# Issuing the context stream's weight loads from ScalarE's queue instead of SyncE's

## The chip, the cores and the metric

The kernel runs on one core of one Trainium2 chip. The metric is the device time of one execution in microseconds (us), as the median of several runs. Engines are named as in the profile: PE is TensorE's matmul side and PEld its weight load, DVE is VectorE, ACT is ScalarE, POOL is GpSimd, SP is SyncE. SPq and ACTq are the instruction streams of SP and ACT where they issue DMAs.

## The reference

Two blocks run one after the other on a sequence of 256 tokens with D = 1024, all in float32.

```
first block:  h = modulate(rms_norm(x));  x += w_out(dilated attention(h) | differential attention(h))
              h = modulate(rms_norm(x));  x += moe_ffn(h)      # 32 experts, top 4 of them per token, d_ff 1024
              expert:  gu = h @ w_gate_up[e];  g = min(gu_g, 7);  u = clip(gu_u, -7, 7)
                       y  = (g * sigmoid(1.702 g) * (u + 1)) @ w_down[e]
second block: 2 layers over x and a second stream "context" (256 tokens); each layer:
              h = modulate(rms_norm(.)); attention (x also sees the context's K and V),
              a gated MLP branch and a convolution branch, each gated and merged, then w_out;
              then a feed-forward block of 4096 with a squared relu
              the context stream itself is needed through layer 0 only
```

The context's layer 0 does not depend on the first block at all; only the second block's attention needs its K and V.

## The kernel before

A `Builder` class writes the program for a tile scheduler, which places each instruction on its engine's queue by priority and by its own estimate of time. Phase 1 (`build`, from L1766) runs the first block: `front` (attention), `route` (top 4, sort, groups of tokens) and `moe`. While it runs, the whole of the context's layer 0 is put between its steps as filler: `ctx_pass` (L1421) is a generator, and `prio` (L1755) advances it by a listed number of steps (tables FRONT, ROUTE, MOE) behind each step of the first block, whose instructions have the higher priority. While the context's code is written, the flag `self.side` is true (`run_ctx` in `build`). When the generator ends, `self.solo` is set and the experts have the chip alone. Phase 2 then runs the two layers of the main stream, `layer(0)` and `layer(1)`.

In the profiled execution the stages lie so: front 0 to about 285 us, route to about 320, the context beside the experts 345 to 1245, the experts alone 1250 to 1590, the two layers 1590 to the end.

Three helpers carry the context's weights. `load_w` (L317) loads a block of 1024 x 512 float32 weights (2 MB). While `self.side` is true it does so in four DMAs of 512 KB, each into a buffer from `half()` (L297): three of four into one of three `raws` buffers, the fourth into the one `rawx`. The DMA's line is L330, and its queue is `q`, chosen in L319; no caller in the context's code passes one. `wsplit` (L335) makes two operands of each 128 x 512 row of the block: ACT copies it to fp32r as `whis` (L342), and DVE subtracts that from the row to get the rest, `wlos` (L343), with three buffers of each. When both splits of a `raws` buffer's two rows are done, the buffer is free for the next load. `lin_steps` (L354) uses each row in twelve matmuls on PE (L365, tile `side`): for each of four column groups the activation's high part on `whis`, its low part on `whis`, and its high part on `wlos`.

The experts' weights take another road. `load_gu` (L941, DMA at L947) loads an expert's gate and up weights in four DMAs of 2 MB and `load_dn` (L952, DMA at L958) its down weights in two, into two `raw` buffers and one `raw3`, used in turn; all from SP. They are float32 and go to PE without a split: L981 (tile `mlin` or `main`) multiplies gate and up, `swiglu` (L917) runs on DVE (L920 to L925) with one tanh on ACT (L923, tile `et`), PE transposes (L987), ACT copies the result to `aT` (L989), L1006 multiplies by the down weights, and ACT puts the outcome into `y` (L1042). The index of each expert is loaded into a register of SP (`value_load` in `expert_base`), so the experts' DMAs can be issued by SP alone as the code stands.

At the end of phase 1 two blocks of layer 0 are loaded ahead with `self.tail` true and `self.side` false; and phase 2 uses `load_w` with `self.side` false throughout.

Of the kernel before, what the change touches and what calls it, by code (L numbers as in the profile page):

```python
# [98 lines left out]
class Builder:  # L99
# [216 lines left out]

    def load_w(self, w, q=None):  # L317

        q = q or self.nc.sync  # L319
        small = self.side  # L320
        if self.tail:
            self.nblock += 1
            small = self.nblock % 3 == 0
        whole = None if small else self.t(self.raw, [P, 4096], tag="raw")
        rows, k0 = [], 0
        for h in (1, 1, 1, 1) if small else (2, 2):
            n = 2 * h
            r = self.half() if small else whole[:, k0 * 512:(k0 + n) * 512]
            r = r.rearrange("p (k n) -> p k n", k=n)
            q.dma_start(r, w[:, k0:k0 + n, :])  # L330
            rows += [r[:, i:i + self.wn, :] for i in range(0, n, self.wn)]
            k0 += n
        return rows
# [1547 lines left out]
```

## Time and profile before

| | |
|---|---|
| median of 3 runs | 2759.27 us (2755.33 to 2763.97) |
| the profiled execution, its own time | 2754.71 us |
| span from its first to its last instruction | 2752.8 us |
| mean granted clock of TensorE over the span | 0.977 of full speed |
| PE busy | 2592.5 us, 94% of the span |
| DVE, ACT, POOL busy | 1626.1, 1157.5, 322.2 us |
| bytes moved by DMA | 769.80 MB |

The busy times are sums over the whole span; they say nothing yet of which engine sets the pace in which stage. For that, the trace is cut into the stages named above. Waits are listed as pairs: the instruction that waited, then the work that ended its wait.

### The profile page before, as it was taken

What the parts mean: (1) busy time and instruction counts of PE and PEld (TensorE: products, weight loads), DVE (VectorE), ACT (ScalarE), POOL (GpSimd) and SP (SyncE); (2) the same over time, 40 slices, a digit from 0 to 9 for tenths busy, and PEclk for the clock granted to TensorE, in tenths of its full rate; (3) what the DMA queues carried; (4) which work ended last, traced back from release to release, by engine and by line L of the source; (5) the groups of instructions that cost most, each with busy time, mean ns of one, the idle gap of its engine ahead of it and who ended that gap; (6) DMA issues with size and microseconds to landing.
All of it is one profiled execution on the core that took longest, in us unless ns stands there. A gap on an engine that the chain in (4) does not pass through costs nothing. (4 is left out here: it accounts for less than half of the span.)

```text
span 2752.8 us, 49781 instructions
## 1 busy us (share of the span) xinstructions
PE 2592.5 (94%) x20358; PEld 2047.0 (74%) x20359; DVE 1626.1 (59%) x3090; ACT 1157.5 (42%) x1987; POOL 322.2 (12%) x334
## 2 busy tenths in 40 slices
PE   7999999999899999999889978899999998999998
PEld 5657877678567777875333477899789987899998
DVE  3465543778554524443121279988546789996655
ACT  2333343333243323431111156765445566656543
POOL 0000000000000000000000025442001055350000
PEclk9989899999999999999999989999999999999999
DMA  9758599989999999999999934326854443344442
GB/s 398 300 226 296 203 401 417 364 347 405 378 357 386 390 361 361 409 419 363 392 392 421 415 129 168 125 105 238 289 203 184 158 180 123 131 146 184 154 184 85
DMA packets 119370, 769.80 MB, mean 280 GB/s; under 512 B 11632, under 2 KB 12016, under 8 KB 52832
## 3 DMA queue, kind: packets, MB, share of 16 engines
q1 hardware_dynamic: 117744, 759.15, 70.6%
q0 software_dynamic: 1392, 7.41, 0.7%
q8 instruction: 162, 2.65, 0.4%
q14 instruction: 72, 0.59, 0.1%
HBM read 762.84 MB, written 3.67 MB: 278 GB/s over the span
## 5 line engine op out<-in xcount | busy, mean ns | idle before, releaser
L343 DVE TENSOR_TENSOR wlo<-raw,whi 128x1024 fp32r<-128x1024 f32 (+1 forms) x288 | 337.6, 1175 | 162.2 <-ACT whi L342 156.6
L365 PE MATMUL lin<-hhi,wlo 128*128 128x256 f32 x1440 | 399.3, 283 | 21.6 <-DVE wlo L343 21.6
L365 PE MATMUL lin<-hhi,whi 128*128 128x256 f32 x1440 | 400.5, 282 | 2.2 <-ACT hhi L284 2.2
L365 PE MATMUL lin<-hlo,whi 128*128 128x256 f32 x1440 | 401.4, 281 | 0.1
L342 ACT ACTIVATE whi<-raw 128x1024 fp32r<-128x1024 f32 (+1 forms) x288 | 276.9, 963 | 257.9 <-PE lin L365 189.3
L981 PE MATMUL mlin<-raw,hG 128*32 128x256 f32 (+2 forms) x2920 | 341.3, 456 | 17.5 <-DMA raw<-in_w_gate_up_dram 17.5
L365 PEld LDWEIGHTS lin<-hhi,wlo 128*128 128x128 f32 x1440 | 269.5, 190 | 37.5 <-DVE wlo L343 33.2
L1585 POOL TENSOR_TENSOR yc<-yc,ctmp 128x256 f32<-128x256 f32 x240 | 252.4, 1075 | 300.6 <-ACT ctmp L1584 300.1
L343 DVE TENSOR_TENSOR wlos<-raws,whis 128x512 fp32r<-128x512 f32 x246 | 166.2, 687 | 196.3 <-ACT whis L342 189.4
L365 PEld LDWEIGHTS lin<-hhi,whi 128*128 128x128 f32 x1440 | 271.0, 189 | 5.8 <-ACT hhi L284 3.7
L365 PEld LDWEIGHTS lin<-hlo,whi 128*128 128x128 f32 x1440 | 272.2, 189 | 3.7 <-issue 2.3
L981 PEld LDWEIGHTS mlin<-raw,hG 128*32 128x32 f32 (+2 forms) x2920 | 129.9, 121 | 178.6 <-issue 110.0
L342 ACT ACTIVATE whis<-raws 128x512 fp32r<-128x512 f32 x246 | 148.9, 627 | 225.6 <-PE side L365 186.2
L365 PE MATMUL side<-hhi,whis 128*128 128x256 f32 x720 | 203.0, 288 | 0.1
L365 PE MATMUL side<-hlo,whis 128*128 128x256 f32 x720 | 199.7, 282 | 0.0
L365 PE MATMUL side<-hhi,wlos 128*128 128x256 f32 x720 | 193.1, 284 | 0.7 <-DVE wlos L343 0.5
L343 DVE TENSOR_TENSOR wlo<-raws,whi 128x1024 fp32r<-128x1024 f32 x108 | 139.0, 1287 | 74.4 <-ACT whi L342 73.8
L1587 DVE SCALAR_TENSOR_TENSOR yc<-gl,cw,yc 128x256 f32<-128x256 f32 x240 | 167.8, 734 | 0.1
L342 ACT ACTIVATE whi<-raws 128x1024 fp32r<-128x1024 f32 x108 | 114.4, 1059 | 118.8 <-PE lin L365 103.8
L1006 PE MATMUL main<-raw,aT 128*32 128x256 f32 (+2 forms) x1408 | 162.6, 453 | 1.1 <-DMA raw<-in_w_down_dram 1.0
L365 PEld LDWEIGHTS side<-hhi,whis 128*128 128x128 f32 x720 | 136.7, 190 | 16.5 <-issue 11.2
L365 PE MATMUL lin<-ahi,whi 128*128 128x256 f32 x528 | 145.7, 279 | 0.0
(603 smaller groups left out, 5737.4 us busy)
## 6 DMA issues: line engine op xcount, KB each, us to landing
raw<-in_w_gate_up_dram SPq DMA_DIRECT2D x120, 2048.0 KB, 11.5
raw<-in_w_down_dram SPq DMA_DIRECT2D x55, 2048.0 KB, 11.1
raw<-in_w_in_dram SPq DMA_DIRECT2D x60, 1024.0 KB, 7.1
raws<-in_w_in_dram SPq DMA_DIRECT2D x95, 512.0 KB, 6.8
raws<-in_w_ff_dram SPq DMA_DIRECT2D x88, 512.0 KB, 8.1
raw<-in_w_ff_dram SPq DMA_DIRECT2D x44, 1024.0 KB, 7.0
phi<-in_ada_w_dram SPq DMA_DIRECT2D x10, 1024.0 KB, 7.4
plo<-in_ada_w_dram SPq DMA_DIRECT2D x10, 1024.0 KB, 7.1
```

What stands on the lines that cost most here:

```text
L342: x = nc.scalar.activation(flat(hi), flat(rows[i]), AF.Copy)
L343: y = nc.vector.tensor_sub(flat(lo), flat(rows[i]), flat(hi).bitcast(F32))
L365: x = nc.tensor.matmul(*args, skip_group_check=True, **kw)
L981: nc.tensor.matmul(d, hT(k), gu[k][c0 // D][:, c0 % D:c0 % D + W], start=False, stop=(k == KC - 1), skip_group_check=True)
L1006: nc.tensor.matmul(pys[h][g * C:(g + 1) * C, :W], st, dn[m][:, c0:c0 + W], start=(m == 0), stop=(m == KC - 1), skip_group_check=True)
L1585: nc.gpsimd.tensor_add(d, d, m)
L1587: self.paced(1, nc.vector.scalar_tensor_tensor(d, x, wcol, d, op0=OP.mult, op1=OP.add))
```

## The change

One line of `load_w` is altered: where no queue is passed and `self.side` is true, the DMA is issued by ACT instead of SP.

```diff
     def load_w(self, w, q=None):
 
-        q = q or self.nc.sync
+        q = q or (self.nc.scalar if self.side else self.nc.sync)
         small = self.side
```

41 calls of `load_w` are made with the flag set, so 164 DMAs of 512 KB (84 MB) change queue. SP's queue goes from 995 instructions to 831, ACT's from 1807 to 1974. The loads of the experts, of the main stream, and of the two blocks loaded ahead stay on SP.

On SP, early in the context stream, the loads of the context's weights (L330) stood between those of the experts (L947, L958; the ISA rows are the register work for the expert's address). The piece of the difference:

```order
 L947 ISA
 L947 DMA raw_6020<-in_w_gate_up_dram 128x2x2048
-L330 DMA raws_3181<-in_w_attn_o_dram 128x1024
-L330 DMA raws_3183<-in_w_attn_o_dram 128x1024
 L947 ISA
 L947 DMA raw_1240_6022<-in_w_gate_up_dram 128x2x2048
-L330 DMA rawx_3185<-in_w_attn_o_dram 128x1024
-L330 DMA raws_3442<-in_w_in_dram 128x1024
 L947 ISA
 L947 DMA raw_6024<-in_w_gate_up_dram 128x2x2048
 L958 ISA
 L958 DMA raw_6112<-in_w_down_dram 128x4096
```

The experts' loads now stand behind one another, and each waits for its own buffer only.

On ACT, at the same place, the splits `whis` of the context's weights (L342) stood so before, each with what it waits for (DMAHW is the arrival of a load, DVE and PE a count of work on these engines):

```order
L342 ACTIVATE whis_3189<-raws_3179 128x512 [waits DMAHW0_49,DVE_49]
L342 ACTIVATE whis_3205<-raws_3179 128x512 [waits DVE_49]
L342 ACTIVATE whis_3221<-raws_3181 128x512 [waits DMAHW2_49,DVE_49]
L342 ACTIVATE whis_3237<-raws_3181 128x512 [waits DVE_49,PE_49]
L342 ACTIVATE whis_3253<-raws_3183 128x512 [waits DMAHW3_49,DVE_49,PE_49]
L342 ACTIVATE whis_3269<-raws_3183 128x512 [waits DVE_49,PE_49]
```

and after the change:

```order
L342 ACTIVATE whis_3189<-raws_3179 128x512 [waits DMAHW0_49]
L342 ACTIVATE whis_3205<-raws_3179 128x512
L330 DMA raws_3442<-in_w_in_dram 128x1024 [waits DMAHW7_49,DVE_49]
L342 ACTIVATE whis_3221<-raws_3181 128x512 [waits DMAHW2_49]
L342 ACTIVATE whis_3237<-raws_3181 128x512 [waits PE_49]
L342 ACTIVATE whis_3253<-raws_3183 128x512 [waits DMAHW3_49,PE_49]
L330 DMA raws_3444<-in_w_in_dram 128x1024 [waits DMAHW1_49,DVE_49]
L342 ACTIVATE whis_3269<-raws_3183 128x512 [waits PE_49]
L330 DMA raws_3446<-in_w_in_dram 128x1024 [waits DVE_49]
```

The load that refills a buffer (`raws_3442` takes that of `raws_3179`) has come in behind the split that empties it, and waits for DVE's half of that split; the splits behind it on ACT wait with it. Of the 160 loads on ACT for which such a split is found, 51 stand directly behind it, 62 one instruction later and 47 further on; 100 are followed at once by another split, 11 by the tanh of L923, 7 by the copy of L989 and 8 by that of L1042. The eight arrival semaphores (DMAHW0 to DMAHW7) are given out in turn to the loads of both queues, and a load waits until the one that had its semaphore before it has landed: 77 of ACT's loads wait on one of SP's, and 74 of SP's on one of ACT's.

On PE the scheduler has laid the experts' steps otherwise between the context's matmuls. At the first matmuls of one expert that read `raw_7604`, in the middle of the context stream, before (`side` is a context matmul; the pair of L981 stands twice in both orders and is shown once):

```order
L365 MATMUL side_6162<-phi_3853,whis_6220 128x256
L365 MATMUL side_6162<-plo_3854,whis_6220 128x256
L365 MATMUL side_6162<-phi_3853,wlos_6221 128x256
L981 MATMUL mlin_7612<-raw_7604,hG_6939 32x256 x4
L981 MATMUL mlin_7613<-raw_7604,hG_6939 32x256 x4
L365 MATMUL side_6161<-phi_3853,whis_6239 128x256
```

and after the change:

```order
L365 MATMUL side_5706<-hlo_640,whis_5840 128x256
L365 MATMUL side_5706<-hhi_639,wlos_5841 128x256
L1006 MATMUL main_7415<-raw_1435_7413,aT_7245 32x256 x16
L981 MATMUL mlin_7612<-raw_7604,hG_6939 32x256 x4
L981 MATMUL mlin_7613<-raw_7604,hG_6939 32x256 x4
L365 MATMUL side_6161<-phi_3853,whis_6163 128x256
```

This expert's matmuls stand 48 context matmuls earlier than before. Over eight experts in a row there the shift is 15, 23, 48, 56, 8, 47, 33 and 56, a mean of 36; at the end of the context stream it is 0, after some experts that stand up to 24 later. Behind that, and in all of phase 2, the order is as before on every engine.

## Rows read from the trace of the kernel before

**Rows 1.** The page: span, busy time by engine, and the DMA queues used

```profile
span 2752.8 us, 49781 instructions
PE 2592.5 (94%) x20358; PEld 2047.0 (74%) x20359; DVE 1626.1 (59%) x3090; ACT 1157.5 (42%) x1987; POOL 322.2 (12%) x334
...
q1 hardware_dynamic: 117744, 759.15, 70.6%
```

**Rows 2.** Busy time by stage: stretch, length, busy PE, PEld, DVE, ACT, POOL, PEclk, DMA share, GB/s

```profile
345.00:1245.00 900.00, 878.25 (x7868) 660.79 (x7869) 478.42 (x1018) 324.00 (x623) 10.96 (x24) 0.98 0.96 384
1250.00:1590.00 340.00, 299.11 (x1491) 132.90 (x1490) 74.37 (x158) 42.71 (x73) 3.34 (x8) 0.97 0.97 394
1590.00:2755.00 1165.00, 1090.37 (x8747) 1022.16 (x8746) 897.61 (x1318) 669.92 (x1043) 298.76 (x274) 0.98 0.45 163
```

**Rows 3.** Waits of SP's queue, 345 to 1245: us in total, times, longest us

```profile
SPq L330 <- DVE wlos L343: 298.2, 117, 6.4
SPq L947 <- PE main L1006: 142.2, 36, 10.8
SPq L947 <- PE mlin L981: 123.1, 36, 7.0
SPq L958 <- PE mlin L981: 105.8, 34, 6.9
SPq L958 <- PE side L365: 12.3, 3, 7.9
```

**Rows 4.** The experts' loads, lines L947 and L958, 345 to 1245: ns min/median/max, first and last

```profile
L947 SPq DMA_DIRECT2D raw<-in_w_gate_up_dram x83: 372/393/427, 348.0 to 1239.8; - x83
...
DMA to landing us min/median/max: 7.3/11.5/17.8
...
L958 SPq DMA_DIRECT2D raw<-in_w_down_dram x42: 333/343/379, 360.9 to 1233.3; - x42
...
DMA to landing us min/median/max: 7.5/11.1/17.4
```

**Rows 5.** The context's weights, tile raws, 345 to 1245: ns min/median/max, first and last

```profile
L342 ACT ACTIVATE whis<-raws x224: 611/631/642, 345.6 to 1242.3; 128x512 fp32r<-128x512 f32 x112
L343 DVE TENSOR_TENSOR wlos<-raws,whis x224: 674/691/695, 347.3 to 1242.9; 128x512 fp32r<-128x512 f32 x112
L330 SPq DMA_DIRECT2D raws<-in_w_ff_dram x48: 327/328/418, 865.5 to 1226.7; - x48
...
DMA to landing us min/median/max: 4.1/9.9/17.8
```

**Rows 6.** Waits of ACT and of DVE, 345 to 1245: us in total, times, longest us

```profile
ACT whis L342 <- PE side L365: 234.5, 135, 7.7
ACT y L1042 <- PE main L1006: 54.1, 17, 9.8
ACT et L923 <- DVE eg L920: 45.4, 19, 9.9
...
DVE wlos L343 <- ACT whis L342: 233.0, 141, 8.3
```

**Rows 7.** Waits of PE and PEld for expert weights, 345 to 1245

```profile
PE mlin L981 <- DMA raw<-in_w_gate_up_dram: 6.4, 3, 4.3
...
PEld mlin L981 <- DMA raw<-in_w_gate_up_dram: 7.6, 3, 4.8
```

**Rows 8.** Timeline of PE, three context matmuls at 917 us: start us, duration us

```profile
917.07 0.28 PE L365 MATMUL side<-hhi,wlos 128*128 128x256 f32 x1
917.18 0.28 PE L365 MATMUL side<-hhi,whis 128*128 128x256 f32 x1
917.29 0.28 PE L365 MATMUL side<-hlo,whis 128*128 128x256 f32 x1
```

**Rows 9.** Busy time of two short stretches, columns as in Rows 2

```profile
620.00:690.00 70.00, 68.62 (x724) 57.00 (x725) 58.18 (x126) 24.64 (x46) 0.82 (x2) 1.00 1.00 404
690.00:760.00 70.00, 61.96 (x526) 41.03 (x526) 40.55 (x101) 16.41 (x34) 0.58 (x2) 0.90 0.94 379
```

## The prediction, made before the changed kernel was run

> **What bounds the kernel now.** I read the page first, for the span and the queues [rows 1], then busy time by stage [rows 2], then, in the stretch that the change touches, the waits of the engine that sets the pace and of the queues that feed it.
>
> The moved loads are issued while the context stream runs beside the first block, and nearly all of their splits lie in 345 to 1245. There PE is busy 878.25 of 900 us, so that only 21.75 us are idle, while ACT is busy 324.00 (36%), DVE 478.42 (53%) [rows 2]. PE waited for expert weights three times, 6.4 us [rows 7]. So PE's work bounds this stretch, with DMA close behind at a share of 0.96. From 1250 to 1590 the share is 0.97 with PE at 299.11 of 340 us: DMA bounds that stretch, and none of its loads changes queue. From 1590 on the order is as before on every engine. [...]
>
> **What SP is relieved of.** A load on SP could be late for two reasons: its own buffer is not free, or the load queued ahead of it waits. The rows tell them apart, since a load held only by its predecessor follows at once, with no wait of its own. The context's loads waited 117 times for DVE's half of the split that empties their buffer, 298.2 us in all [rows 3]. Of the 83 + 42 = 125 expert loads [rows 4], three rows alone show 36 + 36 + 34 = 106 that waited for the PE matmul which last read their buffer [rows 3]. So at most 19 expert loads came late through a load ahead of them. Of what that cost, PE shows at most the 6.4 us of waits for weights. I take half, **−3 us**, since a load may also land late for the bytes ahead of it; the ends are 0 and −6.4.
>
> The issue itself costs SP 0.33 us a load, 164 x 0.328 = 54 us [rows 5], but SP does no other work than to issue, and sat waiting for longer than this in each of the first three rows of [rows 3]. That saving is worth nothing.
>
> The context's loads themselves may land sooner if they no longer stand behind 2 MB of expert weights: 9.9 us in the median now, 4.1 at best [rows 5]. It is worth something only where PE waited for them. ACT, before a split, waited mostly for PE to give back a `whis` buffer, 234.5 us [rows 6], and that is the opposite of late data. [...]
>
> Whether a second queue changes how bytes share the engines, no row shows: one hardware queue carried all of the loads [rows 1]. [...]
>
> **What ACT takes on.** The 164 loads cost ACT the same 0.328 us each, taken from [rows 5] since no row shows a load issued by ACT: **54 us** of issue. Besides, each waits for DVE's half of the split that empties its buffer. For the 51 loads that stand directly behind ACT's half of it, that is a full DVE split, 0.691 us [rows 5], or 35 us; the 62 that stand one instruction later are past it mostly, since that instruction is itself a split of 0.631. Together 54 + 35 = 89 us of ACT's time, where ACT has 576 idle.
>
> Does it reach PE? One row of weights is twelve context matmuls, each 0.11 us after the last [rows 8], 1.36 us. A load's two rows give PE 2.7 us of work, more where expert matmuls lie between. ACT needs for them 2 x 0.631 + 0.328 = 1.59, and 2.28 where it waits for DVE; so ACT still keeps up with PE. And the splits come early: 135 of 224 waited for PE, 234.5 / 135 = 1.74 us each [rows 5, 6], where the load in front of them costs 0.33 to 1.02. Most of the 89 us is hidden in that idle time. What cover remains gone: where the instruction right behind the load is not a split but a step of an expert, which has no queue of finished operands: 11 + 7 + 8 = 26 tanhs, copies to `aT` and copies to `y`. The ends for these are 0, if context matmuls fill PE meanwhile, and 26 x 1.02 = 27 us; by the issue alone it is 26 x 0.33 = 8.6. I take **+5 us**, nearer to the lower end, because the tanh and the copy to `y` themselves waited for DVE and PE, 45.4 us in 19 and 54.1 us in 17 [rows 6], so a load often lies in that wait.
>
> **What else moves.** A load also waits for the arrival of the one eight earlier that had its semaphore, now often one of the other queue. In 900 us there are 125 expert loads and about 149 of the context (224 / 2 of `raws` and a third more of `rawx` [rows 5]), one per 3.3 us, eight per 26 us, and the slowest landed after 17.8 [rows 4, 5]: nothing, unless loads bunch. The experts' matmuls stand up to 56 context matmuls earlier in the middle. PE's total work is the same, so this costs nothing as long as their weights have landed; 0 is taken, and the price if not is a rival.
>
> **The sum.** Profiled execution 2754.71 − 3 + 5 = 2756.7. The median of the runs lies 2759.27 − 2754.71 = 4.6 above it, so **2761 us**, no difference that a measurement can tell: that takes about 0.3%, 8 us.
>
> **The rivals.** *ACT is held at its queue's head (slower).* A load that waits for DVE or for a semaphore holds every split, tanh and evacuation behind it. For it: 224 − 135 = 89 splits, 40%, did not wait for PE, so they had no margin of that kind; and DVE waited for ACT's split 141 times, 233.0 us [rows 6], so a late split is passed on at once. If 40% of the cost is exposed, it is 0.40 x 54 = 22 us for the issue alone and 0.40 x 89 = 35 with the waits: 2781 to 2794, **2788** taken. Against it: the three `whis` buffers put ACT up to two rows, 2.7 us, ahead. It decides where the hold exceeds the 1.74 us.
>
> *Experts come before their weights (slower).* A mean of 36 context matmuls x 0.113 = 4.1 us earlier, eight times, would be 33 us if each expert waited that long, and 56 x 0.113 = 6.3 if the first wait puts all later ones right. For it: expert loads take up to 17.8 us [rows 4], and the DMA share is 1.00 in 620 to 690 [rows 9], so nothing can bring them sooner. Against: PE lacked weights for only 6.4 us before [rows 7]. The middle is about +17: **2776**. It decides once weights land less than 4 us ahead of their use.
>
> [...]
>
> *The change separates nothing.* If the shared semaphores tie the two queues as firmly as one queue did, the landing times of both kinds stay as in [rows 4, 5], and only ACT's cost is left, 2764; it falls into the forecast.
>
> **How the numbers follow.** Forecast (with the last rival) 0.40; ACT held 0.22; experts too early 0.13; loads past the experts' 0.25. The forecast lies within 0.3%, the second and third beyond it on the slow side, the last on the fast one: faster 0.25, same 0.40, slower 0.35. The range goes from 2740, which leaves out only the far end of the fast case, to 2790, which leaves out the upper third of the held one. The forecast's own range is 2752 to 2768, by its ends −6 and +9.
>
> **What would show it.** Right: PE idle in 345 to 1245 stays near 22 us; ACT's waits for PE before `whis` shrink from 234.5 by some 50 to 90 us and turn into issue time and waits of ACTq for `wlos`; DVE's waits for `whis` change little. Held: PEld waits for `whis` and `wlos` appear as tens of us, and the stretch ends after 1270. Experts too early: PE L981 waits for gate and up weights well above 6.4 us, between 500 and 900. [...] I am wrong as a whole if the time from 1590 on, or the experts alone, changes by more than a few us.

## The result, and the profile of the changed kernel

| | before | changed |
|---|---|---|
| median | 2754.49 us (16 runs) | 2772.36 us (16 runs, 2768.99 to 2788.45) |
| ratio to before | | 1.0078, 95% interval 1.0063 to 1.0093 |
| the profiled execution, its own time | 2754.71 us | 2782.27 us |
| a second profiled execution | | 2773.38 us |

The change makes the kernel slower by 0.78%, 21 us by this ratio (the medians lie 17.9 us apart, the means 21.4). That is inside the range, but not the "no difference" that was forecast. The first profile of the changed kernel lies 10 us above its median, the second 1 us.

The page of the changed kernel: there is now a second hardware queue, q10, with the 86 MB of the context's loads (MB are counted in millions here), beside [rows 1]:

```profile
span 2780.3 us, 49602 instructions
## 1 busy us (share of the span) xinstructions
PE 2604.5 (94%) x20358; PEld 2059.7 (74%) x20359; DVE 1629.1 (59%) x3090; ACT 1160.5 (42%) x1987; POOL 327.9 (12%) x334
...
q1 hardware_dynamic: 94128, 673.15, 61.8%
q10 hardware_dynamic: 23616, 85.99, 8.1%
```

Busy time by stage of the changed kernel, columns as in [rows 2]:

```profile
345.00:1245.00 900.00, 868.52 (x7727) 656.18 (x7719) 469.20 (x1005) 321.73 (x614) 13.19 (x24) 0.97 0.93 373
...
1590.00:2755.00 1165.00, 1099.13 (x8707) 1021.08 (x8706) 896.76 (x1313) 666.85 (x1037) 300.01 (x272) 0.98 0.46 169
```

PE's idle time in 345 to 1245 rose from 21.75 to 900 − 868.52 = 31.5 us and its clock fell from 0.98 to 0.97, so the loss begins where the change acts. How much of it lies there is best read from the stage's own length: from the first to the last split of a `rawx` buffer. This row, of the view of the tile `whis`, is used for every run below; its two last times are those of the first and last start. In the kernel before:

```profile
L342 ACT ACTIVATE whis<-rawx x82: 613/632/637, 273.1 to 1251.2; 128x512 fp32r<-128x512 f32 x82
```

and in the changed kernel:

```profile
L342 ACT ACTIVATE whis<-rawx x82: 615/632/636, 271.7 to 1273.1; 128x512 fp32r<-128x512 f32 x82
```

The stage took 978.1 us before and 1001.4 after (993.0 in the second profile): 15 to 23 us more. The spans of these executions are 27.5 and 18.6 us longer (2780.3 and 2771.4 for 2752.8), so all but 4 us of the loss lies in this stage. The two profiles of one kernel also say how far a single reading of the stage can be trusted: they differ by 8.4 us.

What PE waited for there in the changed kernel, beside [rows 7] (us in total, times, longest):

```profile
PE mlin L981 <- DMA raw<-in_w_gate_up_dram: 9.6, 4, 3.3
PE mlin L1036 <- DVE eg L920: 9.2, 3, 7.8
PE side L365 <- ACT whis L342: 2.5, 3, 1.2
```

The second row was 0.2 us in the kernel before: now PE once stood 7.8 us until DVE had read an expert's sums in L920. PE's waits for the context's splits, which a blocked ACT would bring, are 2.5 us. And SP's queue in the changed kernel, beside [rows 3]:

```profile
SPq L947 <- PE main L1006: 270.8, 36, 20.3
SPq L958 <- PE mlin L981: 221.9, 36, 12.4
SPq L947 <- PE mlin L981: 177.7, 36, 17.5
```

SP now waits longer in each, 670 us for 371, since it has nothing else to do, but for the same work of PE and as often (108 times for 106). So at most a few of the experts' loads had been held back by the loads ahead of them.

### The profile page after: what moved, and what is told of

It is laid out like the page before. It is cut to its first block, busy times and chain, and to the rows that moved or that the text cites. A ratio compares the mean times of both kernels' runs of the same rounds, so it can differ in the third digit from the quotient of the medians.

```text
span 2780.3 us, 49602 instructions
## 1 busy us (share of the span) xinstructions
PE 2604.5 (94%) x20358; PEld 2059.7 (74%) x20359; DVE 1629.1 (59%) x3090; ACT 1160.5 (42%) x1987; POOL 327.9 (12%) x334
## 5 line engine op out<-in xcount | busy, mean ns | idle before, releaser
L365 PE MATMUL lin<-hhi,wlo 128*128 128x256 f32 x1440 | 400.2, 284 | 19.2 <-DVE wlo L343 18.8
L365 PE MATMUL lin<-hhi,whi 128*128 128x256 f32 x1440 | 401.5, 282 | 2.2 <-ACT hhi L284 2.2
L365 PE MATMUL lin<-hlo,whi 128*128 128x256 f32 x1440 | 403.0, 282 | 0.0
L342 ACT ACTIVATE whi<-raw 128x1024 fp32r<-128x1024 f32 (+1 forms) x288 | 277.1, 964 | 257.9 <-PE lin L365 188.3
L981 PE MATMUL mlin<-raw,hG 128*32 128x256 f32 (+2 forms) x2920 | 341.8, 458 | 22.4 <-DMA raw<-in_w_gate_up_dram 22.3
L365 PEld LDWEIGHTS lin<-hhi,wlo 128*128 128x128 f32 x1440 | 271.4, 191 | 34.7 <-DVE wlo L343 30.6
L365 PEld LDWEIGHTS lin<-hlo,whi 128*128 128x128 f32 x1440 | 274.4, 191 | 4.3 <-issue 2.3
L365 PEld LDWEIGHTS lin<-hhi,whi 128*128 128x128 f32 x1440 | 273.1, 191 | 5.6 <-ACT hhi L284 3.7
L981 PEld LDWEIGHTS mlin<-raw,hG 128*32 128x32 f32 (+2 forms) x2920 | 130.4, 121 | 183.7 <-issue 108.2
L342 ACT ACTIVATE whis<-raws 128x512 fp32r<-128x512 f32 x246 | 150.6, 627 | 203.9 <-PE side L365 160.0
L365 PE MATMUL side<-hhi,whis 128*128 128x256 f32 x720 | 203.6, 289 | 1.2 <-ACT whis L342 1.2
L365 PE MATMUL side<-hlo,whis 128*128 128x256 f32 x720 | 199.1, 282 | 0.0
L365 PE MATMUL side<-hhi,wlos 128*128 128x256 f32 x720 | 189.5, 283 | 0.7 <-DVE wlos L343 0.4
L1587 DVE SCALAR_TENSOR_TENSOR yc<-gl,cw,yc 128x256 f32<-128x256 f32 x240 | 172.9, 756 | 0.1
L342 ACT ACTIVATE whi<-raws 128x1024 fp32r<-128x1024 f32 x108 | 114.5, 1060 | 128.0 <-PE lin L365 96.4
L365 PEld LDWEIGHTS side<-hhi,whis 128*128 128x128 f32 x720 | 137.1, 190 | 16.7 <-issue 12.5
L1020 POOL CAST pick<-sel 128x288 fp32r<-128x288 f32 (+1 forms) x32 | 17.4, 544 | 1118.0 <-PE mlin L1036 1017.4
```

The source lines that it names most:

```text
L342: x = nc.scalar.activation(flat(hi), flat(rows[i]), AF.Copy)
L365: x = nc.tensor.matmul(*args, skip_group_check=True, **kw)
L981: nc.tensor.matmul(d, hT(k), gu[k][c0 // D][:, c0 % D:c0 % D + W], start=False, stop=(k == KC - 1), skip_group_check=True)
L1020: nc.gpsimd.tensor_copy(pick.rearrange("p (c n) -> p c n", c=n), src.unsqueeze(2).to_broadcast([P, n, w]))
L1587: self.paced(1, nc.vector.scalar_tensor_tensor(d, x, wcol, d, op0=OP.mult, op1=OP.add))
```

## The experiments

The change does three things at once: ACT has 164 more instructions and their waits, the loads have a queue of their own (and share their arrival semaphores with SP's loads across the two queues), and the scheduler lays out all engines anew. To take these apart, the scheduler's order was pinned. A table holds the order of another build for the first part of the program, a row each for PE, DVE, ACT and POOL, and each instruction is tied to its forerunner on its engine by a dependency that sets the order of issue and waits for nothing. The loads are not in the table; they are fitted in by the scheduler. With the new order and all loads on SP, the experts' loads therefore stand up to two context loads earlier or later in SP's queue than before; with the old order and all loads on SP, at most one.

```diff
+def pin(tc, nc):
+    ins = nc.cur_bb.bb.instructions
+    for text in PINS:
...
+            if prev is not None:
+                tc.add_manual_dep(ins[k], ins[prev].name, mybir.DependencyInfo(
+                    mybir.DependencyClass.NoSync, mybir.DependencyReason.DATA), reason="order")
```

The first theory was that the new order costs the time; its rivals were ACT held at its queue's head, and the sharing of the DMA engines between two queues. Each run below was made 3 to 12 times, beside the kernel before; the stage is that of its one profiled execution, 978.1 us in the kernel before.

| run | order | context's loads | ratio to before (95%) | stage, us |
|---|---|---|---|---|
| changed kernel, second profile | new | ACT | 1.0071 (1.0050 to 1.0092) | 993.0 |
| oldorder_actq | old | ACT | 1.0039 (1.0022 to 1.0055) | 986.5 |
| neworder_spq | new | SP | 1.0052 (1.0034 to 1.0071) | 987.1 |
| oldorder_poolq | old | POOL | 1.0033 (1.0019 to 1.0048) | 986.1 |
| oldorder_actburden | old | SP, ACT burdened | 0.9999 (0.9982 to 1.0016) | 975.6 |
| oldorder_onefifo_pool | old | POOL, with the experts' | 1.0058 (1.0038 to 1.0077) | 978.8 |
| oldorder_twoqueues | old | ACT and POOL in turn | 1.0053 (1.0035 to 1.0070) | 994.7 |
| neworder_until830_spq | new, then old | SP | 1.0006 (0.9989 to 1.0023) | 982.2 |
| neworder_from830_spq | old, then new | SP | 1.0012 (0.9992 to 1.0032) | 980.7 |

### The queue without the order

The changed line, with the pins of the kernel before.

> The loads are on ACT's queue as in the change, but PE, DVE, POOL and the arithmetic on ACT are pinned to the order of the kernel before; the loads alone are fitted in among ACT's instructions. Order theory (the loss of about 18 us comes from experts' steps that the scheduler has put ahead of their weights and ahead of their place on DVE, each with a dip of the clock behind it): back to the time before, ratio 0.998 to 1.002. Held-ACT theory (splits and tanhs wait behind loads on ACT): the loss stays, ratio 1.005 to 1.009, with PE and PEld waits for whis and wlos well above the 8 us of before. Queue-sharing theory (context loads on a queue of their own take bandwidth from the experts' loads that were issued earlier): ratio 1.002 to 1.008, with PE waits at L981 for gate and up weights above 10 us.

Half of the loss stayed, 0.39%. The splits are not what PE waits for; the experts' weights are (waits of PE in this run, 345 to 1245):

```profile
PE mlin L981 <- DMA raw<-in_w_gate_up_dram: 12.4, 6, 3.8
PE side L200 <- DVE sqs L254: 2.2, 3, 0.8
```

12.4 us for 6.4 before: the queue-sharing theory's case. The experts' gate and up loads of the whole stretch also land later than before [rows 4], by 0.6 us in the median and 1.8 at the end:

```profile
DMA to landing us min/median/max: 7.5/12.1/19.6
```

### The order without the queue

The line as before, with the pins of the changed kernel.

> The mirror image: all loads stay on SP as in the kernel before, but PE, DVE, POOL and ACT are pinned to the order that the changed kernel has. Order theory: the loss is here in full, ratio 1.005 to 1.009, with holes of several us on PE near 345 and 720 us. Held-ACT and queue-sharing theories: nothing of what they need is present, ratio 0.998 to 1.002.

A loss of 0.52% needs no second queue; the intervals do not tell whether this part or the other is the larger. PE's timeline in this run, where the number in brackets is the idle time ahead and what ended it:

```profile
711.64 3.66 PE L981 MATMUL mlin<-raw,hG 128*32 128x256 f32 x64
...
723.25 0.77 PE L1036 MATMUL mlin<-bgh,pick 128*128 128x512 f32 x1 [7.94 <-DVE eg L920]
```

and DVE's at the same time:

```profile
715.13 1.27 DVE L1587 SCALAR_TENSOR_TENSOR y<-gl,cw,y 128x256 f32<-128x256 f32 x3
716.32 0.68 DVE L1658 TENSOR_TENSOR m<-m,g 128x512 f32<-128x512 f32 x1
716.92 0.48 DVE L1587 SCALAR_TENSOR_TENSOR y<-gl,cw,y 128x256 f32<-128x256 f32 x1
717.32 0.68 DVE L1658 TENSOR_TENSOR m<-m,g 128x512 f32<-128x512 f32 x1
717.92 3.25 DVE L1587 SCALAR_TENSOR_TENSOR y<-gl,cw,y 128x256 f32<-128x256 f32 x8
721.09 0.68 DVE L343 TENSOR_TENSOR wlos<-raws,whis 128x512 fp32r<-128x512 f32 x1
721.69 0.47 DVE L1587 SCALAR_TENSOR_TENSOR y<-gl,cw,y 128x256 f32<-128x256 f32 x1
722.09 0.68 DVE L343 TENSOR_TENSOR wlos<-raws,whis 128x512 fp32r<-128x512 f32 x1
722.69 0.41 DVE L920 TENSOR_SCALAR eg<-mlin 128x256 f32<-128x256 f32 x1
```

The expert's matmuls are done at 715.3, but its L920 stands on DVE behind the rest of the context's convolution (L1587) and merge (L1658), 7 us of work without a gap. In the kernel before, the expert's last matmuls ended 4.3 us later, and L920 stood 1.4 us earlier:

```profile
716.10 3.48 PE L981 MATMUL mlin<-raw,hG 128*32 128x256 f32 x32 [4.32 <-DMA raw<-in_w_gate_up_dram]
...
721.26 0.41 DVE L920 TENSOR_SCALAR eg<-mlin 128x256 f32<-128x256 f32 x1
```

In the new order the next expert's L1036 needs the buffer of sums that L920 empties, and all that follows on PE stands behind it. Windows of this run show what comes after (columns as in [rows 2]):

```profile
710.00:720.00 10.00, 5.30 (x80) 3.40 (x78) 10.00 (x25) 1.78 (x3) 0.00 (x0) 0.87 1.02 417
720.00:730.00 10.00, 5.53 (x22) 4.74 (x22) 7.63 (x19) 0.61 (x2) 0.00 (x0) 0.50 1.01 422
730.00:740.00 10.00, 10.00 (x92) 7.14 (x94) 1.26 (x4) 1.18 (x3) 0.43 (x1) 0.78 0.21 86
```

In the ten microseconds in which the hole ends the granted clock is 0.50, and 0.78 in the ten after; PE counts as busy there, but takes longer for the same work: sixteen matmuls of L1629 at 725.67 took 3.58 us, for 1.95 at 720.21 in the kernel before. In the kernel before PE is idle in the same stretch too, 5.9 us for weights, and the clock falls as well [rows 9]; over 690 to 760 it is 61.96 us busy at 0.90 there, and 59.40 at 0.85 here. So of the hole's 8 us about 2.6 are extra idle time, and 70 x 0.05 = 3.5 us extra clock: by this estimate some 6 us for this place.

Of the 17.4 us by which this profiled execution is longer than the one before (spans 2770.2 and 2752.8 us), 9.0 lie in the stage; 2.1 lie ahead of it and 6.3 behind it, where the order is that of before. In the other runs with all loads on SP what lies behind the stage is between 3.9 us shorter and 4.1 longer than before, so part of the 17.4 may be no more than the scatter of single executions.

### Is it ACT?

The pins and the queue of the kernel before; ACT writes into the buffer ahead of each load.

```diff
             r = r.rearrange("p (k n) -> p k n", k=n)
+            if self.side:
+                self.extra.add(self.nc.scalar.activation(r[:, 0, 0:P], self.ident, AF.Copy).ins.name)
             q.dma_start(r, w[:, k0:k0 + n, :])
```

> Order and queue of the kernel before, but ahead of each context load ACT writes 128 columns into the buffer to be loaded, so that ACT has 164 more instructions of about 0.3 us, each waiting for DVE's half of the split that empties the buffer, at nearly the places where the loads stand on ACT's queue. No second queue and no new order. Held-ACT theory: the same loss as with the loads themselves there, ratio 1.005 to 1.009. Order and queue-sharing theories: ratio 0.998 to 1.002. My own forecast had 5 us for this burden, ratio 1.002.

It costs nothing, which also shows that the pins by themselves cost nothing, and the burden was there: the added instructions (0.31 us each), and ACT's waits in this run (three lines are added above, so its L332 is the new instruction, L345 the split):

```profile
L332 ACT ACTIVATE raws<-cst x111: 292/310/317, 345.5 to 1226.6; 128x128 f32<-128x128 f32 x111
```

```profile
ACT whis L345 <- PE side L368: 177.1, 132, 7.6
ACT raws L332 <- DVE wlos L346: 66.7, 58, 6.0
...
ACT rawx L332 <- DVE wlos L346: 29.6, 22, 7.1
```

ACT waited 96.3 us for DVE, and its wait for PE ahead of the splits fell from 234.5 [rows 6] to 177.1. The time was taken out of the cover.

The same from the other side: the loads on POOL's queue, old order, `self.nc.gpsimd` in the changed line.

> Order of the kernel before, context loads on POOL's queue, which has next to nothing to do in this stretch. Order theory: ratio 0.998 to 1.002. Held-ACT theory: ACT is free of the loads, 0.998 to 1.002. Queue-sharing theory: a second queue is there as with ACT's, so whatever the run with ACT's queue and the old order loses must be lost here too, or won if small loads get past large ones (PE idle in 690 to 760 below 8 us, ratio 0.995).

0.33%, as with ACT's queue, with ACT untouched. The held-ACT theory is out by both runs; what costs is the second queue. Nor can it be the arrival semaphores that the two queues share in the change: in this run's trace POOL's loads have eight of their own, and the loss is the same. PE's waits for gate and up weights are longer still here:

```profile
PE mlin L981 <- DMA raw<-in_w_gate_up_dram: 16.4, 11, 4.6
```

### What the second queue does

The view of the DMA queues and issues, 685 to 706 us, where the DMA engines are busy throughout (a share of 101.2% and 100.0% in the two views). Columns of the queues: packets, MB, share of 16 engines; of the issues: number, KB each, median us from issue to landing. In the kernel before:

```profile
q1 hardware_dynamic: 1451, 8.77, 101.2%
...
raw<-in_w_gate_up_dram SPq DMA_DIRECT2D x3, 2048.0 KB, 14.8
raws<-in_w_in_dram SPq DMA_DIRECT2D x3, 512.0 KB, 15.3
```

in the run with ACT's queue and the old order:

```profile
q1 hardware_dynamic: 716, 6.09, 69.8%
q10 hardware_dynamic: 694, 2.53, 30.2%
...
raw<-in_w_gate_up_dram SPq DMA_DIRECT2D x3, 2048.0 KB, 16.4
raws<-in_w_in_dram ACTq DMA_DIRECT2D x3, 512.0 KB, 9.3
rawx<-in_w_gmlp_o_dram ACTq DMA_DIRECT2D x1, 512.0 KB, 13.2
rawx<-in_w_in_dram ACTq DMA_DIRECT2D x1, 512.0 KB, 11.7
```

With one queue each of the seven loads landed 14.0 to 16.2 us after its issue, large or small, and in the order of issue: they were issued at 688.8 to 703.5 and landed at 703.6 to 718.6. With two, the context's loads landed after 9.3 to 13.2 us and the experts' after 16.4. The two queues moved nearly the same number of packets, 716 and 694 (748 and 699 with POOL's queue). So the second queue changed which loads landed first, and the two runs with it and the old order lost 0.3 to 0.4%.

Two runs test this. In the first, the context's and the experts' loads are together on POOL's queue while the context runs:

```diff
-        q = q or (self.nc.scalar if self.side else self.nc.sync)
+        q = q or (self.nc.gpsimd if self.side else self.nc.sync)
...
-        reg = nc.sync.value_load(self.ids[0:1, i:i + 1], min_val=0, max_val=NE - 1)
+        eng = nc.sync if self.solo else nc.gpsimd
+        reg = eng.value_load(self.ids[0:1, i:i + 1], min_val=0, max_val=NE - 1)
```

> Order of the kernel before; while the context runs, the context's loads and the experts' loads are both issued by POOL, so that there is one queue again, in which a load is served behind those issued before it, but not SP's. Queue-sharing theory (what costs is that context loads on a queue of their own are served ahead of expert loads issued earlier): the loss of the run with POOL for the context alone is gone, ratio 0.998 to 1.002, and the context's loads land in about 10 us in the median again, as late as the experts' beside them. Rival (what costs is that POOL issues them more slowly or with other descriptors): ratio 1.003 or more.

As a ratio this missed: 1.0058, which is what the rival foretold (1.003 or more). By stage it did not. The context's stage is 978.8 us, for 978.1 before, and both kinds of load land after 15 us again (685 to 706). PE's waits for weights, the last line here, are little more than before:

```profile
L342 ACT ACTIVATE whis<-rawx x82: 614/632/637, 275.8 to 1254.6; 128x512 fp32r<-128x512 f32 x82
```

```profile
q0 software_dynamic: 1329, 8.72, 100.4%
...
raw<-in_w_gate_up_dram POOLq DMA_DIRECT2D x3, 2048.0 KB, 15.0
raws<-in_w_in_dram POOLq DMA_DIRECT2D x2, 512.0 KB, 15.4
```

```profile
PE mlin L981 <- DMA raw<-in_w_gate_up_dram: 8.7, 5, 4.3
```

One stage of one execution is a weak witness by itself, since the changed kernel's own two differ by 8.4 us. But the runs fall into two groups: with the old order the stage is 975.6 to 978.8 us in the three executions with one queue, and 986.1 and 986.5 in the two with two.

The 16 us that this run loses by its ratio lie outside that stage: in its profiled execution, 14.6 us longer than the one before, 2.7 lie ahead of the stage and 11.2 behind it. There it has two queues again: POOL still issues the experts' loads until 1426 us, and SP, with nothing ahead of it, starts on four blocks of later experts at 1259 to 1278, which the kernel before loads only from 1408 on, behind the others. That these got ahead of earlier ones fits the theory, but was not tried by itself, and neither was the rival that POOL issues more slowly (0.71 us a load for SP's 0.39).

In the second run the context's loads go to ACT's and POOL's queues in turn, so that three queues contend:

```diff
-            q.dma_start(r, w[:, k0:k0 + n, :])
+            p = (self.nc.scalar, self.nc.gpsimd)[k0 // 2 % 2] if self.side else q
+            p.dma_start(r, w[:, k0:k0 + n, :])
```

> Order of the kernel before; the context's loads are issued in turn by ACT and by POOL, so that beside SP's queue of expert loads there are two others. Queue-sharing theory: a larger share for the context where the queues contend, so a larger loss than with one such queue, ratio 1.004 to 1.008, with the experts' loads later than in that run. Rival (a second queue costs a fixed amount, or the loss is ACT's or POOL's own): 1.003 to 1.004 as with one.

0.53%, and in the profiled execution the stage is 994.7 us: +16.6, twice the +8.4 and +8.0 of the runs with one extra queue. But this execution took 2781.66 us, 14.6 above the median of its kernel, so part of the 16.6 is its own. The experts' gate and up loads landed after 17.3 us (685 to 706), for 16.4 with ACT's queue and 17.0 with POOL's:

```profile
q1 hardware_dynamic: 575, 6.31, 71.5%
q10 hardware_dynamic: 375, 1.41, 16.6%
q0 software_dynamic: 289, 1.05, 12.5%
...
raw<-in_w_gate_up_dram SPq DMA_DIRECT2D x3, 2048.0 KB, 17.3
```

The intervals of the ratios of one and two extra queues overlap, and the landing times hardly differ, so that two extra queues cost more than one is not shown. What the runs with the old order show is that an extra queue costs time, whichever engine issues on it (0.39% from ACT, 0.33% from POOL). That it does so by changing which loads land first rests on the landing times (with ACT's queue 16.4 and 9.3 us, for 14.8 and 15.3), on PE's waits for gate and up weights (12.4 and 16.4 us, for 6.4) and on the stage of the run with one queue on POOL (978.8 us).

### Where in the order

The changed kernel once more, then the new order in halves. The cut is a point at which PE, DVE and ACT have each done the same set of instructions in both orders.

> The changed kernel once more, for a second profile of it. Order theory: the hole of about 8 us on PE near 720 us, ended by DVE's L920, is there again, since the order is the same. Queue-sharing theory: the waits at L981 for gate and up weights are again longer than before, though not at the same places to the microsecond.

The hole at 720 was there again (9.2 us in three waits, the longest 7.3), and so were the waits at L981, 8.3 us in five.

> All loads on SP. Pinned orders: that of the changed kernel up to a point at about 830 us at which PE has done the same set of instructions in both, and that of the kernel before from there on. If the order's loss comes from two places, the convolution's end at 700 to 755 us and the norms at 850 to 930 us, as the two traces put side by side say (6 us each), this run holds the first: ratio 1.002 to 1.003, with the 8 us hole ended by DVE's L920 and without the smaller holes at 900 to 933. Rival (the loss is one mechanism, such as experts being early everywhere): not divided so.

> The other half: the order of the kernel before up to that point at about 830 us and that of the changed kernel from there on, loads on SP. Two-places theory: ratio 1.002 to 1.003, without the 8 us hole near 720, with the small holes at 855 to 933 and the clock below 0.8 in 900 to 930. The two ratios less 1 should add up to about 0.005.

Both ratios missed the 1.002 to 1.003 that was expected, and neither is told from zero by its interval. In 720 to 730, where the hole lies, PE is idle 5.4 us in the first half and 2.0 in the second (0.9 before, 4.5 with the whole order), as expected, and the clock is 0.50 and 0.65 in 900 to 920 of the second (0.68 and 0.81 before). The stages are 4.1 and 2.6 us longer than before, for 9.0 with the whole order. But 0.06 + 0.12% is not 0.52%; with errors of some 0.2% on each of the three the gap is about as large as their error together. That the order costs some 0.5% is shown; that it does so in these two places and nowhere else is not.

No run came out faster than the kernel before.

## Why the prediction was right and wrong

**The bound** was right. PE's work sets the context's stage, and the loss lies there: from the last split to the end it is 1501.6 us before, and 1507.2 and 1504.2 in the two profiles after. The 5.6 us of the first are at the edge of the "few us" that were to tell of an error; other single executions scatter by some 4 us there. How large a gain could have been was never tested, since nothing was gained.

**SP's relief, "I take half, −3 us"**: the sign was wrong. The argument that SP's loads hardly held each other up holds; SP waits for the same work as before. What it missed is that one queue was also an order of landing. The experts' loads, for which PE waits, landed in the order of issue with one queue, 14.8 us after it at 685 to 706; with two they took 16.4 us, and the context's small loads, which have time, landed after 9.3 instead of 15.3. What a second queue does, which no row of before showed, measured +0.39% (ACT's queue, old order), 0.0039 x 2754.6 = 11 us, with 6 to 15 from its interval. The chance of 0.25 for loads past the experts', and the range down to 2740 with it, had the wrong sign: no run shows a gain from this. The context's loads did land earlier and the experts' later, and PE waited for one kind almost alone: with ACT's queue and the old order 12.4 us for the experts' gate and up weights, and 0.5 for the context's splits. The rival of the shared semaphores, that the landing times would stay, is out by the same rows.

**ACT's burden, "+5 us"**: measured 0 within 5 us either way (0.9999, ±0.0017). The issue cost 0.334 us, for 0.328 taken. The cover by ACT's idle time ahead of the splits was complete; the upper end of 27 us and the rival at 2788 are excluded by the run with the burden alone. (The forecast's own range had left that end of 27 out without a word, and gone by the 8.6 of the issue.)

**The order, "0 is taken"**: this step failed most. It measured +0.52%, 0.0052 x 2754.6 = 14 us, with 9 to 20 from its interval. The price was given to the second rival, at 2776 (the middle of its 6.3 and 33 would have been 2779), but by another mechanism, weights that have not landed. With the order alone the largest wait is on DVE: an expert whose matmuls end 4.3 us earlier on PE meets an L920 that did not move up with it. By the estimate above that place is some 6 us; where the rest of the 14 lies is open. Late weights come in as well: in the changed kernel PE stood 3.3 us at 341 (the longest such wait of the second profile is 2.8) for a block that landed after 18.3 us. With the order alone PE was idle 1.3 us in 330 to 340 and 1.1 in 340 to 350; whether the queue alone brings such a wait there was not shown.

**The sum**: 11 + 14 = 25 us by the parts, 21 measured for both; by the stage 8.4 + 9.0 = 17.4 us, with 15 to 23 measured. The forecast had −3 + 5 + 0. That the time still lies in the range is luck: the range reached so far up for the held ACT, which the runs with the old order exclude, and neither of the two causes found was in the sum.

**The signs to look for**: ACT's wait for PE did shrink, to 206.5 us in the changed kernel, but by 28 and not 50 to 90. One sign of the held ACT appeared without its cause, a stage that ends after 1270 (1273.1 in the first profile); the other, tens of us of PEld's waits for `whis` and `wlos` at L365, did not (11.3, for 7.9 before). The landing of `raws` over the whole stage hid the effect: 9.9 before, 9.5 after. In 685 to 706, at a DMA share of 101.2%, it is 15.3 before and 9.3 with ACT's queue and the old order.

## What to carry to other kernels

In this kernel a load's queue was also its place in line: with one queue large and small loads landed 14.8 and 15.3 us after their issue, with two 16.4 and 9.3. Before small loads that have time are moved to a queue of their own, ask which loads PE waits for, and whether these then land later; here one queue, with landings in the order of issue, was better than two by 0.3 to 0.4%. And where a scheduler lays out the program, a one-line change is two changes: pin the old order to see the one, and pin the new order without the change to see the other.

## What had not been expected of the hardware

With ACT's queue and the old order, two queues moved 716 and 694 packets in 21 us, 6.09 and 2.53 MB: nearly equal in packets, but not in bytes. The packets of SP's queue are larger, 6.09 MB / 716 = 8.5 KB for 3.6 KB, so the queue with large packets kept 70% of the engines' time; still, the large loads landed 7 us later after their issue than the small ones, 16.4 and 9.3 in the median. With three queues the packets were 575, 375 and 289; why these differ, and how two queues come to nearly equal numbers, no run here shows. And with the new order and all loads on SP the ten microseconds in which a hole of 8 us on PE ended had a granted clock of 0.50, the next ten 0.78.
